# A hybrid decoder trunk on one core: the rectified index scores of a head stay in their bank of PSUM

## The chip, the cores and the metric

The kernel runs on one core of a Trainium2 chip. The metric is the device time of one execution in microseconds. A core has a matrix engine (TensorE, rows "PE" for matmuls and "PEld" for weight loads), an elementwise engine (VectorE, "DVE"), an engine for pointwise functions (ScalarE, "ACT"), a general engine (GpSimd, "POOL") and one that issues most DMAs here (SyncE, "SP"). Each works off its own queue in order and waits for the others at semaphores. SBUF is the working memory; PSUM holds what TensorE writes, in eight banks of 128 partitions x 512 float32.

## The reference, cut to what matters

The model has two layers on an input of 512 tokens x 1024 features. Layer 0 mixes stick-breaking attention with an S5 state space model; layer 1 is a sparse attention that picks 128 keys for each query by an "index score". Each mixer is followed by a squared-ReLU MLP, and both are wrapped as x <- LN(alpha x + f(x)). The change touches the index scores of layer 1:

```python
def block(args):
    q_b, qi_b, wi_b, bid = args
    tpos = bid * Q_BLOCK + jnp.arange(Q_BLOCK)
    rel = jax.nn.relu(jnp.einsum('bqhd,bsd->bqsh', qi_b, ki).astype(jnp.float32))
    score = jnp.einsum('bqsh,bqh->bqs', rel, wi_b.astype(jnp.float32)) * idx_scale
    causal = (spos[None, :] <= tpos[:, None])[None]
    score = jnp.where(causal, score, -jnp.inf)
    _, idx = lax.top_k(score, topk)
```

There are 8 index heads (`IDX_HEADS`) of 32 features, four blocks of 128 queries, and `topk` is 128. The picked keys then go through a softmax attention with 16 heads on 4 key/value heads and a distance penalty (ALiBi).

## The kernel before, in words

All matmuls with weights run three times on a split of each float32 into a high and a low part (`mm3`, L129 to L133). In layer 1 (`mixer_dsa`, L957) the work is issued in this order:

- `index_scores` (L1017) projects the index queries, keys and head weights, carries them through DRAM into the stacked tiles `qist` and `kist`, and calls `score_block` (L1078) for the query blocks 1, 2 and 3. Block 0 needs no choice, since it sees only 128 keys.
- `score_block` handles one block of 128 queries against nk = 256, 384 or 512 keys. For each of the 8 heads TensorE makes one matmul into a bank (`psx`, L1086), ScalarE writes the rectified scores into an SBUF tile `rel` (L1088; the tag has four buffers, and `wiT` in L1062 uses the same tag), and VectorE adds `rel` times the head's weight to the accumulator `acc` in SBUF (L1089). The first addition takes the mask `cm` in place of `acc`.
- `top_keys` (L1114) picks the 128 largest scores of a block on VectorE: 16 steps, each a MAX8 (L1121) and a MATCH_REPLACE8 with its value load (L1122). Then L1126 and L1127 turn the marks into the distance tile `dist`. It is called for block 1, then for block 2, and for block 3 behind the attention of the other blocks in the program's order.
- `project_v1` (L1093) and two `proj_fm` calls make values and keys, and eight `project_q` calls (L1006) make the query pairs. Each `project_q` takes its weights through L104 (ScalarE) and L105 (GpSimd from the third pair on, else VectorE), and its result through L864 and L865 (ScalarE), L866 (GpSimd) and four DMAs (L853) into `qst`.
- `sparse_attention` (L1129) makes the logits of a head (`psl`, L1144), adds the distances on VectorE (L1151, a custom operation that reads `psl` in PSUM and `dist` in SBUF), takes Exp on ScalarE (L1153), scales on GpSimd (L1157), transposes (L944, L945) and sums the values (L951).

The banks: `abank` (L76) hands out four banks of PSUM in turn, three of the tag `psa` and one of the tag `psp`. `psx`, some of the `psi` of the projections, and later `psl`, come from these four. A bank is free again when the last instruction that uses its tile is done. The other four banks (tag `psb`) serve the projections of keys, values and queries.

The order of each engine's queue is not written by hand. The program is traced in the order above, which gives each instruction its priority, and a planner lays out the queues by its own model of time: on every engine the instruction of highest priority whose inputs and buffers are free at that moment goes next. So a queue holds work of several steps mixed: among the projections TensorE finds the matmuls of the scores, and VectorE finds additions between top-k steps. On the chip the queues run in that fixed order.

Of the kernel before, what the change touches and what calls it, by code (L numbers as in the profile page):

```python
# [8 lines left out]
F32 = mybir.dt.float32  # L9
F32R = mybir.dt.float32r  # L10
AF = mybir.ActivationFunctionType
# [4 lines left out]
P = 128  # L16
S = 512
# [18 lines left out]
class Trunk:  # L36
# [1041 lines left out]
    def score_block(self, qb, wi, qst, kst, cm, op, ip):  # L1078

        nc = self.nc  # L1080
        nk = (qb + 1) * P
        qs = slice(qb * P, (qb + 1) * P)
        acc = op.tile([P, S], F32, tag="acc", bufs=3, name=self.nm("acc"))[:, :nk]
        for h in range(8):
            ps = self.abank([P, S], "psx")
            nc.tensor.matmul(ps[:, :nk], qst[:, h, qs], kst[:, :nk], start=True, stop=True)  # L1086
            r = ip.tile([P, S], F32, tag="rel", bufs=4, name=self.nm("rel"))[:, :nk]
            nc.scalar.activation(r, ps[:, :nk], AF.Relu)  # L1088
            nc.vector.scalar_tensor_tensor(acc, r, wi[:, qb, h:h + 1], acc if h else cm[:, S - nk:],  # L1089
                                           ALU.mult, ALU.add)  # L1090
        return acc
# [118 lines left out]
```

## Time and profile before

| | us |
|---|---|
| median of 3 runs (1156.58 to 1158.6) | 1157.38 |
| the profiled execution, its own time | 1157.72 |
| its span, first to last instruction | 1155.9 |
| TensorE matmul busy | 1113.2 (96%) |
| TensorE weight load busy | 928.3 (80%) |
| VectorE busy | 839.0 (73%) |
| ScalarE busy | 532.8 (46%) |
| GpSimd busy | 172.4 (15%) |

The shares are means over stages that differ: what is worth something is read from the stage, from the wait that ends last there. The ends of matmuls are modelled, so a busy TensorE need not be at its peak. The stage that the change touches lies between 606 us (first index score) and some 720 us (last of the top-k steps), in which the DMA engines moved data through more than half of the time up to 680 us. [...]

In the rows, "[7.10 <- X]" says how long the engine stood idle before the row's first instruction and what the profile names as its releaser; "x8" says that eight instructions are merged in the row, which then gives the time from the first start to the last end.

### The profile page before, as it was taken

How to read it: one execution, taken by the hardware profiler on the slowest of the kernel's cores; microseconds unless marked ns; L12 is line 12 of the kernel's file. 1: busy time of each engine (PE TensorE's matmuls, PEld its weight loads, DVE VectorE, ACT ScalarE, POOL GpSimd, SP SyncE). 2: the span in 40 equal slices, each digit the busy share in tenths (PEclk: the TensorE clock that was granted, in tenths of full speed). 3: DMA queues.
4: the chain of work that ended last, by engine and by line, in shares of the span. 5: the costliest groups of instructions: out<-in, count | busy, mean ns of one | idle time of the engine just before them, and what ended most of it. 6: DMA issues, size and time to landing. Idle time of an engine off the chain costs nothing.

```text
span 1155.9 us, 15562 instructions
## 1 busy us (share of the span) xinstructions
PE 1113.2 (96%) x5860; PEld 928.3 (80%) x5860; DVE 839.0 (73%) x1255; ACT 532.8 (46%) x832; POOL 172.4 (15%) x201
## 2 busy tenths in 40 slices
PE   7988999999999999999999979998999999999997
PEld 6877877788888888888898867776988888888886
DVE  7997498695666866975578998556648678587736
ACT  5534387424454544554135446552445444445520
POOL 1043230230000000000121655325000000000001
PEclk9998999999999999999999989998999999999999
DMA  7526683661242242333046960008304405315101
GB/s 247 141 57 155 188 215 117 179 186 38 73 147 90 75 147 71 108 111 79 1 129 159 221 178 1 2 4 271 110 19 128 144 21 162 111 41 160 37 1 73
DMA packets 147307, 126.99 MB, mean 110 GB/s; under 512 B 24353, under 2 KB 115297, under 8 KB 147233
## 3 DMA queue, kind: packets, MB, share of 16 engines
q1 hardware_dynamic: 145552, 123.59, 37.1%
q10 hardware_dynamic: 1680, 2.41, 0.6%
q8 instruction: 46, 0.75, 0.3%
q14 instruction: 29, 0.23, 0.1%
HBM read 105.80 MB, written 5.37 MB: 96 GB/s over the span
## 4 chain that ended last, share of the span: by engine, by line
PE 86%; DVE 7%; DMA 3%; issue 2%; ACT 1%; SPq 1%; POOL 0%; POOLq 0%; DVEq 0%; ACTq 0%
PE psa L132 12%; PE psa L133 12%; PE psa L131 12%; PE psb L313 7%; PE psb L314 7%; PE psb L312 7%; PE pso L951 3%; PE pst L944 3%; PE psb L383 3%; PE psb L382 3%; PE psb L384 3%; PE psb L843 2%; PE psl L1144 2%; PE psb L844 2%; PE psb L845 2%
## 5 line engine op out<-in xcount | busy, mean ns | idle before, releaser
L133 PE MATMUL psa<-xhi,wlo 128*128 128x512 f32 (+1 forms) x720 | 266.9, 371 | 0.0
L132 PE MATMUL psa<-xlo,whi 128*128 128x512 f32 (+1 forms) x720 | 266.6, 371 | 0.0
L131 PE MATMUL psa<-xhi,whi 128*128 128x512 f32 (+1 forms) x720 | 265.2, 371 | 0.2 <-ACT xhi L202 0.2
L104 ACT CAST whi<-raw 128x1024 fp32r<-128x1024 f32 (+1 forms) x129 | 133.6, 1046 | 206.9 <-PE psa L132 127.0
L105 DVE TENSOR_TENSOR wlo<-raw,whi 128x1024 fp32r<-128x1024 f32 (+1 forms) x102 | 128.1, 1260 | 86.8 <-ACT whi L104 86.0
L132 PEld LDWEIGHTS psa<-xlo,whi 128*128 128x128 f32 x720 | 135.7, 188 | 23.3 <-DVE xlo L203 0.4
L133 PEld LDWEIGHTS psa<-xhi,wlo 128*128 128x128 f32 x720 | 135.7, 188 | 22.9
L131 PEld LDWEIGHTS psa<-xhi,whi 128*128 128x128 f32 x720 | 134.8, 188 | 23.3 <-ACT xhi L202 0.5
L313 PE MATMUL psb<-wlo,whi 128*128 128x512 f32 x336 | 130.7, 389 | 0.0
L312 PE MATMUL psb<-whi,whi 128*128 128x512 f32 x336 | 130.7, 389 | 0.0
L300 DVE TENSOR_TENSOR wlo<-b,whi 128x1024 fp32r<-128x1024 f32 x84 | 102.6, 1221 | 38.4 <-ACT whi L299 38.2
L314 PE MATMUL psb<-whi,wlo 128*128 128x512 f32 x336 | 129.8, 389 | 0.0
L299 ACT CAST whi<-b 128x1024 fp32r<-128x1024 f32 x84 | 88.3, 1051 | 41.9 <-PE psb L314 30.2
L105 POOL TENSOR_TENSOR wlo<-raw,whi 128x1024 fp32r<-128x1024 f32 x27 | 69.7, 2592 | 137.8 <-ACT whi L104 136.7
L184 POOL TENSOR_TENSOR rs<-rs,two 128x1 f32<-128x1 f32 x16 | 22.7, 1419 | 418.8 <-DVE rs L183 418.8
L312 PEld LDWEIGHTS psb<-whi,whi 128*128 128x128 f32 x336 | 63.1, 188 | 13.2
L313 PEld LDWEIGHTS psb<-wlo,whi 128*128 128x128 f32 x336 | 63.1, 188 | 13.1
L314 PEld LDWEIGHTS psb<-whi,wlo 128*128 128x128 f32 x336 | 63.1, 188 | 13.0
L294 DVE TENSOR_TENSOR b<-b,b 128x1024 f32<-128x1024 f32 x48 | 58.3, 1221 | 11.1 <-DMA b<-in_w_dram 10.7
L299 ACT CAST whi<-h 128x1024 fp32r<-128x1024 f32 x36 | 37.9, 1054 | 54.0 <-PE psb L313 34.0
L300 DVE TENSOR_TENSOR wlo<-h,whi 128x1024 fp32r<-128x1024 f32 x36 | 44.0, 1221 | 14.0 <-ACT whi L299 13.5
L843 PE MATMUL psb<-whi,xhi 128*128 128x512 f32 x128 | 51.4, 409 | 0.2 <-DVE x L848 0.2
(263 smaller groups left out, 1973.0 us busy)
## 6 DMA issues: line engine op xcount, KB each, us to landing
raw<-in_w_dram SPq DMA_DIRECT2D x80, 512.0 KB, 4.1
b<-in_w_dram SPq DMA_DIRECT2D x48, 512.0 KB, 4.3
raw<-in_w_in_dram SPq DMA_DIRECT2D x29, 512.0 KB, 4.6
raw<-in_w_out_dram SPq DMA_DIRECT2D x16, 512.0 KB, 4.7
qst<-hl SPq DMA_DIRECT2D x48, 128.0 KB, 3.1
kst<-hl SPq DMA_DIRECT2D x24, 256.0 KB, 4.7
gb<-in_ln_g_dram SPq DMA_DIRECT2D x4, 512.0 KB, 4.1
gb<-in_ln_b_dram SPq DMA_DIRECT2D x4, 512.0 KB, 5.1
```

The costliest lines, as they stand in the source:

```text
L104: nc.scalar.copy(hi[:, c], raw[:, c])
L105: (eng or nc.vector).tensor_tensor(lo[:, c], raw[:, c], hi[:, c].bitcast(F32), ALU.subtract)
L131: mm(ps, lhi, rhi, start=start, stop=False)
L132: mm(ps, lhi, rlo, start=False, stop=False)
L133: mm(ps, llo, rhi, start=False, stop=stop)
L294: vec.tensor_tensor(o, p, q, op)
L299: act.copy(hi, src)
L300: vec.tensor_tensor(lo, src, hi.bitcast(F32), ALU.subtract)
L312: mm(ps, lh, bhi[:, k, :], start=i + k == 0, stop=False)
L313: mm(ps, lh, blo[:, k, :], start=False, stop=False)
L314: mm(ps, ll, bhi[:, k, :], start=False, stop=i + k == 2)
L843: nc.tensor.matmul(ps, chi[:, k, tok], whi, start=i == 0, stop=False)
```

## The change

The tile `rel` goes. ScalarE rectifies the scores in place, in the bank that TensorE wrote, and VectorE reads them from there:

```diff
@@ -1084,8 +1084,8 @@
         for h in range(8):
             ps = self.abank([P, S], "psx")
             nc.tensor.matmul(ps[:, :nk], qst[:, h, qs], kst[:, :nk], start=True, stop=True)
-            r = ip.tile([P, S], F32, tag="rel", bufs=4, name=self.nm("rel"))[:, :nk]
-            nc.scalar.activation(r, ps[:, :nk], AF.Relu)
+            r = ps[:, :nk]
+            nc.scalar.activation(r, r, AF.Relu)
             nc.vector.scalar_tensor_tensor(acc, r, wi[:, qb, h:h + 1], acc if h else cm[:, S - nk:],
                                            ALU.mult, ALU.add)
         return acc
```

The numbers of instructions stay as they are: 24 matmuls, 24 rectifications, 24 additions. A bank of `psx` is now in use until VectorE has added it, and no longer until ScalarE has rectified it. The tag `rel` keeps its four buffers, for `wiT`.

## Rows read from the trace of the kernel before

**Rows 1.** From the page, the chain of work that ended last: shares of the span by engine.

```profile
PE 86%; DVE 7%; DMA 3%; issue 2%; ACT 1%; SPq 1%; POOL 0%; POOLq 0%; DVEq 0%; ACTq 0%
```

**Rows 2.** Waits of TensorE's matmuls from 606 to 700 us: in total, times, the longest.

```profile
PE psl L1144 <- DMA qst<-hl: 7.1, 1, 7.1
```

**Rows 3.** The chain of waits from 660 to 700 us: start, us, what.

```profile
684.72 3.98 DMA qst<-hl
688.70 6.24 PE psl L1144 x24
```

**Rows 4.** The timeline from 679 to 690 us, of all engines: start, us, engine, line, operation, tiles, count, and the idle time before with its releaser.

```profile
680.02 1.56 PE L1144 MATMUL psl<-kst,qst 128*128 128x384 f32 x8
688.68 6.26 PE L1144 MATMUL psl<-kst,qst 128*128 128x384 f32 x24 [7.10 <-DMA qst<-hl]
688.68 1.46 PEld L1144 LDWEIGHTS psl<-kst,qst 128*128 128x128 f32 x5 [7.42 <-DVE pst L1151]
...
682.29 1.28 ACT L1153 ACT_TABLE_LOAD   x1
684.22 0.69 DVE L1121 MAX8 top<-acc 128x8 f32<-128x512 f32 x1
685.74 0.69 DVE L1121 MAX8 top<-acc 128x8 f32<-128x512 f32 x1
688.06 0.56 DVE L1151 CUSTOM_DVE_ANT_0 pw<-psl,dist 128x384 f32<-128x384 f32 x1
```

**Rows 5.** All waits of VectorE from 622.5 to 688 us.

```profile
DVE wlo L105 <- ACT whi L104: 0.8, 1, 0.8
```

**Rows 6.** The timeline of VectorE, additions of the scores alone (L1089), blocks 2 (384 keys) and 3 (512 keys).

```profile
627.11 0.61 DVE L1089 SCALAR_TENSOR_TENSOR acc<-rel,wi,acc 128x384 f32<-128x384 f32 x1
627.97 0.60 DVE L1089 SCALAR_TENSOR_TENSOR acc<-rel,wi,acc 128x384 f32<-128x384 f32 x1
...
630.66 2.37 DVE L1089 SCALAR_TENSOR_TENSOR acc<-rel,wi,acc 128x384 f32<-128x384 f32 x1
633.80 0.92 DVE L1089 SCALAR_TENSOR_TENSOR acc<-rel,wi,cm 128x512 f32<-128x512 f32 x1
...
637.03 2.55 DVE L1089 SCALAR_TENSOR_TENSOR acc<-rel,wi,acc 128x512 f32<-128x512 f32 x1
640.88 0.74 DVE L1089 SCALAR_TENSOR_TENSOR acc<-rel,wi,acc 128x512 f32<-128x512 f32 x1
...
643.92 2.54 DVE L1089 SCALAR_TENSOR_TENSOR acc<-rel,wi,acc 128x512 f32<-128x512 f32 x1
```

**Rows 7.** The timeline of GpSimd in the same stretch.

```profile
630.17 2.44 POOL L105 TENSOR_TENSOR wlo<-raw,whi 128x1024 fp32r<-128x1024 f32 x1 [37.21 <-ACT whi L104]
632.57 1.60 POOL L866 TENSOR_TENSOR hl<-ev,hl 128x512 fp32r<-128x512 f32 x1
636.60 2.43 POOL L105 TENSOR_TENSOR wlo<-raw,whi 128x1024 fp32r<-128x1024 f32 x1 [2.42 <-ACT whi L104]
...
643.04 2.88 POOL L105 TENSOR_TENSOR wlo<-raw,whi 128x1024 fp32r<-128x1024 f32 x1 [2.30 <-ACT whi L104]
```

**Rows 8.** The timeline of GpSimd and VectorE from 776 to 800 us.

```profile
786.46 9.09 POOL L105 TENSOR_TENSOR wlo<-raw,whi 128x1024 fp32r<-128x1024 f32 x3 [3.66 <-ACT whi L104]
787.03 2.93 DVE L105 TENSOR_TENSOR wlo<-raw,whi 128x1024 fp32r<-128x1024 f32 x1 [6.36 <-ACT whi L104]
789.88 0.68 DVE L848 SCALAR_TENSOR_TENSOR x<-x,psb 128x512 f32<-128x512 f32 x1
```

**Rows 9.** Four lines of the kernel over the whole span: engine, operation, count, shortest/median/longest in ns, first and last start in us, forms.

```profile
L848 DVE SCALAR_TENSOR_TENSOR x<-x,psb x16: 660/682/689, 179.3 to 812.9; 128x512 f32<-128x512 f32 x16
L105 DVE TENSOR_TENSOR wlo<-raw,whi x102: 683/1222/2927, 6.7 to 1116.9; 128x1024 fp32r<-128x1024 f32 x100, 128x512 fp32r<-128x512 f32 x2
L185 DVE SCALAR_TENSOR_TENSOR x<-x,mv,gb x16: 1271/1276/2425, 233.2 to 1149.7; 128x1024 f32<-128x1024 f32 x16
L1088 ACT ACTIVATE rel<-psx x24: 378/492/606, 607.9 to 639.7; 128x256 f32<-128x256 f32 x8, 128x384 f32<-128x384 f32 x8, 128x512 f32<-128x512 f32 x8
```

**Rows 10.** The timeline of TensorE, the last matmul of a group of four heads, three groups; and of ScalarE, the rectification of the fifth to seventh head of block 3.

```profile
627.96 0.34 PE L1086 MATMUL psx<-kist,qist 96*128 96x384 f32 x1
633.44 0.39 PE L1086 MATMUL psx<-kist,qist 96*128 96x512 f32 x1
638.97 0.40 PE L1086 MATMUL psx<-kist,qist 96*128 96x512 f32 x1
...
637.57 1.74 ACT L1088 ACTIVATE rel<-psx 128x512 f32<-128x512 f32 x3
```

**Rows 11.** The timeline of VectorE, two operations behind the top-k steps.

```profile
648.57 2.60 DVE L1127 TENSOR_TENSOR dist<-acc,drm 128x256 f32<-128x256 f32 x1
670.50 2.35 DVE L1126 TENSOR_SCALAR acc<-acc 128x384 f32<-128x384 f32 x1
```

**Rows 12.** Stretches of the span: length, busy us (and instructions) of TensorE, weight loads, VectorE, ScalarE, GpSimd, then the granted clock, the DMA share and GB/s.

```profile
620.00:640.00 20.00, 20.00 (x98) 16.91 (x97) 19.08 (x39) 14.05 (x25) 7.40 (x4) 1.00 0.54 135
686.00:688.00 2.00, 0.00 (x0) 0.00 (x0) 1.88 (x4) 0.00 (x0) 0.00 (x0) 0.50 0.81 241
...
693.00:694.00 1.00, 1.00 (x7) 1.00 (x6) 1.00 (x6) 0.94 (x4) 1.00 (x2) 0.50 0.00 0
```

## The prediction, made before the result was known

> **What bounds the kernel now.** I read the page's chain of waits first: 86% of it is TensorE's own work, and the profiled execution has a span of 1155.9 us inside its own time of 1157.72 us (1.8 us lie around the span) [rows 1]. So a change can only pay where TensorE stands still. The waits of TensorE between 606 and 700 us show one long one: 7.1 us, in front of the matmuls of the sparse attention (`psl`), put down to a DMA of `qst` [rows 2]. The timeline says otherwise. Eight `psl` matmuls run from 680.02 to 681.58 us and fill the four banks of the score pool; the ninth starts at 688.68 [rows 4]. The chain puts the landing of that DMA at 688.70, after the start it is said to release, and that DMA brings the eighth query pair, while these matmuls read the first four [rows 3]. The weight load of the same moment names VectorE instead, 7.42 us, and VectorE's first `psl` instruction (L1151) begins at 688.06 and ends at 688.62, 0.06 us before TensorE goes on [rows 4]. It frees the first bank. So TensorE waits for VectorE to arrive.
>
> VectorE arrives late because it is full: from 622.5 to 688 us its only wait is 0.8 us [rows 5]. Its queue holds the adding up of the index scores, the top-k steps of blocks 1 and 2, and ten steps of block 3 that the planner put ahead of L1151. Whatever leaves this queue before 688 us moves the attention forward, up to the point where TensorE is the later one: the first two `psl` matmuls are done about 680.5, so at most 7.5 us.
>
> In that queue four of the sixteen score additions of blocks 2 and 3 are stretched. An addition of 128x384 takes 0.60 to 0.61 us and one of 128x512 0.74, but those at 630.66, 637.03 and 643.92 us take 2.37, 2.55 and 2.54, and the one at 633.80 takes 0.92 [rows 6]. Each begins while GpSimd is inside a TENSOR_TENSOR, and the long three end just behind it: 633.03 against 632.61, 639.58 against 639.03, 646.46 against 645.92 [rows 7]. The additions read `rel` and `acc`, both in SBUF.
>
> **The change, part by part.**
>
> *The addition reads PSUM and one SBUF tile.* No row shows this form with a pointer scalar. The nearest is the residual addition L848: same operation, one input in PSUM, 660 to 689 ns, and the one at 789.88 us takes 0.68 in the middle of a GpSimd run of 9.09 us from 786.46, while its neighbour L105, with two inputs in SBUF, takes 2.93 against a median of 1.222 [rows 8, 9]. So I take the stretch as gone: (2.37 - 0.61) + (2.55 - 0.74) + (2.54 - 0.74) + (0.92 - 0.74) = 1.76 + 1.81 + 1.80 + 0.18 = 5.55 us off VectorE's queue. The bounds are 0 (PSUM changes nothing) and 5.55; I take the upper one, since L848 is the same operation under the same GpSimd instruction.
>
> *The unstretched duration.* L848 at 0.682 against 0.735 would make the sixteen additions 16 x 0.05 = 0.8 us shorter; but L848's scalar is an immediate, and a wi column is read per partition. L185, with a pointer scalar, takes 1.276 on 1024 elements where L105 takes 1.222 without one, so 0.05 goes back [rows 9]. I take 0, between -0.8 and +0.8 over the sixteen.
>
> [...]
>
> *The rectifier writes PSUM.* The 24 ScalarE instructions take 378 to 606 ns, PSUM to SBUF [rows 9]; a PSUM output of ScalarE I have no row for. Even 0.1 us either way on each is 2.4 us on an engine that is busy 14.05 of the 20 us from 620 to 640 [rows 12], and the additions behind it wait only where VectorE is already early. I take 0. The four `rel` buffers no longer hold ScalarE back; ScalarE being off the path, that is worth nothing.
>
> *The bank is held longer.* This is the added wait. Before, a bank came free when ScalarE had rectified it; now when VectorE has added it. With four banks, the matmul of head h+4 waits for the addition of head h, and behind it in TensorE's queue stand the projections. Laid against the present order, it hardly bites. The tightest of each four is the last: the eighth matmul of block 2 starts at 627.96, and the addition that would free its bank ends at 627.72; the fourth of block 3 starts at 633.44, where the last addition of block 2, unstretched, ends at 631.27; the eighth starts at 638.97, the addition of the fourth, unstretched, ends at 637.77 [rows 6, 10]. TensorE loses 0 there. VectorE loses something: without stretches it would reach the fifth addition of block 3 at about 640.88 - 3.75 = 637.1, but its rectified bank is only there at 637.57 + 0.6 = 638.17. So 1.07 us of the 5.55 turn into waiting for ScalarE [rows 6, 10]. The planner may place the matmuls earlier or later; between 0 and 2 us lost, I take 1.07.
>
> *Operations that stay stretched.* L1127 and L1126 read SBUF alone; under GpSimd they take 2.60 us at 648.57 and 2.35 at 670.50 [rows 11], some 2 us more each than their size asks for. Moved 4.5 us ahead they begin in another place of GpSimd's rhythm, inside or outside of an instruction. I take 0, between -4 (both free) and +2.
>
> *Sum.* 5.55 - 1.07 = 4.5 us: L1151 begins at about 683.6 and TensorE goes on at 684.2. What is late next is ScalarE: its table load for Exp ends at 683.57, just in time [rows 4]. Everything after follows the same queues in one chain of TensorE pieces, so I let the shift run through to the end. One thing comes on top: the granted clock is 0.50 from 686 to 694 us, after the standstill, and 1.00 from 620 to 640 [rows 12]. The 24 `psl` matmuls behind the standstill take 6.24 us there, where eight took 1.56 at the full clock, which would be 4.7 for 24 [rows 3, 4]; but they also wait for VectorE to free banks, so I expect about 0.5 us of the 1.5 back, between 0 (the clock falls all the same) and 1.5. So 5.0 us: 1157.72 - 5.0 = 1152.7. The profiled execution is 0.34 us above the median of 1157.38 of the runs, so the time is 1152.4 us.
>
> **The rivals.**
>
> *The planner spends the gain (no change).* The order of every queue is written by a planner from its own times. If it thinks VectorE has room before `psl`, it puts more top-k steps of block 3 ahead of L1151. Such a step takes 1.52 us (from one MAX8 at 684.22 to the next at 685.74), and six are left: three more eat 4.6 us, and the time is 1157 [rows 4]. Against it: the stretches look unknown to the planner (L1151 stands where VectorE, without some 10 us of stretches in all, would be at 678, close to `psl`), so removing them need not move its plan.
>
> *The banks become the bound (slower).* Twenty matmuls now wait for an addition. If the planner expects VectorE to be earlier than it is, TensorE stands in front of each. Two such additions start 0.86 us apart (627.11, 627.97) [rows 6]. Its present standstill of 7.1 us is what TensorE can lose before the kernel is slower: 7.1 / 0.86, so from nine matmuls that are reached one step too early, among the sixteen of blocks 2 and 3. With twelve it is 10.3 - 7.1 = 3.2 us: 1160.6. [...] The order of now, laid out above, shows no such early step.
>
> *Half the gain.* One or two steps more ahead of L1151, or PSUM reads that cost 0.05 to 0.1 us more: 5.0 - 2.3 = 2.7, that is 1154.7.
>
> **How the numbers follow.** The forecast gets 0.47, half the gain 0.18, no change 0.19, slower 0.16. A measurement of this kernel tells 0.2% (2.3 us) from no change. Nearly all of the first two cases is faster by more than that, 0.62; same 0.21; slower 0.17. The range reaches down to all of the 7.5 us that VectorE can give back and most of the 1.5 of the clock, 1148.8, and up into the slower case, to 1159.5. The forecast's own range is 1150 to 1154.
>
> **What would show it.** The additions of blocks 2 and 3 all take 0.55 to 0.8 us, those under GpSimd too; L1151 begins about 683.6 and not 688.06; the ninth `psl` follows `psl`'s first eight by under 3 us and not 7.1; the clock falls for a shorter time or not at all. It is wrong if additions from PSUM are stretched as before, if more than ten steps of block 3 stand ahead of L1151, or if TensorE shows waits for `acc` between 620 and 645 us.

## The result, and the profile after

| | before | after |
|---|---|---|
| median (lowest to highest, 4 runs each) | 1157.99 (1156.58 to 1159.16) | 1150.71 (1150.21 to 1152.62) |
| ratio, 95% interval | | 0.9943 (0.9927 to 0.9958) |
| the profiled execution, its own time | 1157.72 | 1151.07 |
| its span | 1155.9 | 1149.3 |
| VectorE busy | 839.0 | 830.8 (72%) |

The change makes the kernel 0.57% faster, 6.6 us between the two profiled executions. The page's chain of waits of the changed kernel, shares of the span by engine, beside [rows 1]:

```profile
PE 88%; DVE 6%; ACT 2%; DMA 1%; issue 1%; SPq 1%; POOL 0%; POOLq 0%; DVEq 0%; ACTq 0%
```

TensorE's share is up by two points and ScalarE's by one, DMA's is down by two; shares of the whole span don't say where the 6.6 us were. That is in the changed kernel's timeline of the stage in front of the attention, all engines, the columns as in [rows 4]:

```profile
680.31 1.91 PE L1144 MATMUL psl<-kst,qst 128*128 128x384 f32 x10
680.86 0.56 DVE L1151 CUSTOM_DVE_ANT_0 pw<-psl,dist 128x384 f32<-128x384 f32 x1 [0.28 <-PE psl L1144]
681.93 1.28 ACT L1153 ACT_TABLE_LOAD   x1
682.55 1.57 PE L1144 MATMUL psl<-kst,qst 128*128 128x384 f32 x6 [0.34 <-DVE pst L1151]
683.23 0.62 ACT L1153 ACTIVATE pw<-pw,pst 128x384 f32<-128x384 f32 x1
...
689.17 0.66 PE L951 MATMUL pso<-pt,v 128*64 128x128 f32 x8 [1.31 <-ACT pt L945]
```

TensorE reaches `psl` at 680.31 (680.02 before), so nothing came from ahead of it. VectorE's L1151 begins at 680.86 and not 688.06, and has now waited 0.28 us for TensorE itself. The standstill of 7.10 us [rows 4] is gone: ten `psl` matmuls run in one piece, and the eleventh waits 0.34. The first Exp begins at 683.23, 0.02 us behind the end of the table load (681.93 + 1.28 = 683.21). Before, it began at 688.66 behind L1151, in the timeline of the kernel before (with its first `pso` matmul, for later):

```profile
688.66 0.62 ACT L1153 ACTIVATE pw<-pw,pst 128x384 f32<-128x384 f32 x1 [5.09 <-DVE pst L1151]
...
696.16 0.66 PE L951 MATMUL pso<-pt,v 128*64 128x128 f32 x8 [0.57 <-ACT pt L945]
```

So 5.43 us of VectorE's 7.2 arrive at ScalarE, and the table load takes the rest. ScalarE is also what ends last behind that. The chain of waits of the changed kernel from 679 to 690 us (start, us, what; "ACT pw" are Exps, each with a read of its sum of 0.19 us behind it):

```profile
681.93 1.28 ACT L1153
...
683.23 0.71 ACT pw L1153 x2
683.94 0.51 ACT hl L865
684.45 4.20 ACT pw L1153 x14
688.65 0.48 ACT pt L945
```

Before, the chain had 6.24 us of TensorE's `psl` matmuls in this place [rows 3]. Now it is ScalarE's table load, eight Exps with one cast of a projection (L865) between them, and a copy, up to the first `pso` matmul.

The additions, in the timeline of the changed kernel's VectorE, for [rows 6]:

```profile
630.36 0.62 DVE L1089 SCALAR_TENSOR_TENSOR acc<-psx,wi,acc 128x384 f32<-128x384 f32 x1 [0.23 <-ACT psx L1088]
...
636.74 0.75 DVE L1089 SCALAR_TENSOR_TENSOR acc<-psx,wi,cm 128x512 f32<-128x512 f32 x1 [0.20 <-ACT psx L1088]
...
643.31 0.75 DVE L1089 SCALAR_TENSOR_TENSOR acc<-psx,wi,acc 128x512 f32<-128x512 f32 x1 [0.40 <-ACT psx L1088]
643.98 0.87 DVE L1126 TENSOR_SCALAR acc<-acc 128x256 f32<-128x256 f32 x1
645.89 0.41 DVE L1127 TENSOR_TENSOR dist<-acc,drm 128x256 f32<-128x256 f32 x1
...
666.69 1.02 DVE L1126 TENSOR_SCALAR acc<-acc 128x384 f32<-128x384 f32 x1
668.24 1.05 DVE L1127 TENSOR_TENSOR dist<-acc,drm 128x384 f32<-128x384 f32 x1
```

And GpSimd in the same time, for [rows 7]:

```profile
629.53 2.41 POOL L105 TENSOR_TENSOR wlo<-raw,whi 128x1024 fp32r<-128x1024 f32 x1 [36.12 <-ACT whi L104]
631.89 1.31 POOL L866 TENSOR_TENSOR hl<-ev,hl 128x512 fp32r<-128x512 f32 x1
635.81 2.41 POOL L105 TENSOR_TENSOR wlo<-raw,whi 128x1024 fp32r<-128x1024 f32 x1 [2.61 <-ACT whi L104]
638.18 1.28 POOL L866 TENSOR_TENSOR hl<-ev,hl 128x512 fp32r<-128x512 f32 x1
642.29 2.41 POOL L105 TENSOR_TENSOR wlo<-raw,whi 128x1024 fp32r<-128x1024 f32 x1 [2.82 <-ACT whi L104]
```

Three additions (630.36, 636.74, 643.31) begin in the middle of a GpSimd subtraction and take 0.62, 0.75 and 0.75 us. Before, such additions took 2.37 to 2.55. Both engines gain: GpSimd's L866 at the first two of these places falls from 1.60 [rows 7] and 1.74 to 1.31 and 1.28. The second of before:

```profile
639.00 1.74 POOL L866 TENSOR_TENSOR hl<-ev,hl 128x512 fp32r<-128x512 f32 x1
```

What the queues wait for. All waits of the matmuls of the changed kernel's TensorE from 618 to 660 us, then VectorE's from 622 to 681 us (in total, times, longest), for [rows 2, 5]:

```profile
PE psx L1086 <- DVE wlo L105: 1.5, 1, 1.5
```

```profile
DVE acc L1089 <- ACT psx L1088: 2.0, 5, 0.7
DVE wlo L105 <- ACT whi L104: 0.5, 1, 0.5
DVE pw L1151 <- PE psl L1144: 0.3, 1, 0.3
```

No matmul waits for `acc`; the one wait, at 621.82, stands ahead of block 2's first scores. VectorE now stands still 2.8 us in all, where it had one wait of 0.8. It is no longer full, and its last wait, in front of L1151, is for TensorE.

One of the stretches of [rows 12] in the changed kernel (the figure behind the five engines is the granted clock of TensorE as a share of its full speed):

```profile
686.00:688.00 2.00, 1.86 (x14) 1.43 (x13) 1.38 (x7) 2.00 (x9) 2.00 (x4) 1.00 0.82 204
```

The clock is 1.00 where it was 0.50 before, and so in every stretch from 606 to 710 us. From the first Exp to the first `pso` matmul it was 688.66 to 696.16, 7.50 us; now it is 683.23 to 689.17, 5.94. As the chain above shows, these 5.94 us are ScalarE's work, no longer TensorE's.

### The profile page after: what moved, and what is told of

It reads as the page before. It is cut to its first block, busy times and chain, and to the rows that moved or that the text cites. A ratio compares the mean times of both kernels' runs of the same rounds, so it can differ in the third digit from the quotient of the medians.

```text
span 1149.3 us, 15542 instructions
## 1 busy us (share of the span) xinstructions
PE 1112.8 (97%) x5860; PEld 926.1 (81%) x5860; DVE 830.8 (72%) x1255; ACT 532.2 (46%) x832; POOL 170.7 (15%) x201
## 3 DMA queue, kind: packets, MB, share of 16 engines
q10 hardware_dynamic: 1680, 2.41, 0.6%
HBM read 105.80 MB, written 5.37 MB: 97 GB/s over the span
## 4 chain that ended last, share of the span: by engine, by line
PE 88%; DVE 6%; ACT 2%; DMA 1%; issue 1%; SPq 1%; POOL 0%; POOLq 0%; DVEq 0%; ACTq 0%
PE psa L133 12%; PE psa L131 12%; PE psa L132 12%; PE psb L313 7%; PE psb L312 7%; PE psb L314 7%; PE pso L951 3%; PE pst L944 3%; PE psb L384 3%; PE psb L383 3%; PE psb L382 3%; PE psb L843 2%; PE psb L844 2%; PE psb L845 2%; PE psl L1144 2%
## 5 line engine op out<-in xcount | busy, mean ns | idle before, releaser
L105 DVE TENSOR_TENSOR wlo<-raw,whi 128x1024 fp32r<-128x1024 f32 (+1 forms) x102 | 128.1, 1260 | 87.3 <-ACT whi L104 86.5
L132 PEld LDWEIGHTS psa<-xlo,whi 128*128 128x128 f32 x720 | 136.2, 189 | 23.5 <-DVE xlo L203 0.4
L105 POOL TENSOR_TENSOR wlo<-raw,whi 128x1024 fp32r<-128x1024 f32 x27 | 69.3, 2576 | 139.0 <-ACT whi L104 137.7
```

The lines of the kernel that those rows point to most:

```text
L105: (eng or nc.vector).tensor_tensor(lo[:, c], raw[:, c], hi[:, c].bitcast(F32), ALU.subtract)
L132: mm(ps, lhi, rlo, start=False, stop=False)
```

## The experiments

Two theories were open. **Theory A**: an addition with two SBUF inputs collides with GpSimd's reads, and a PSUM input ends that. **Theory B**: the gain comes from the new order of the queues, for with other buffers the planner puts eight top-k steps of block 3 ahead of L1151 and not ten, and four steps of block 1 ahead of the first addition of block 2 and not six. (Here and below, steps are counted by their MAX8.)

**e1: the kernel before, GpSimd only writes.** GpSimd's subtractions for six of the query weights (L105) and for the low parts of the keys and queries (L866) become memsets, so these low parts are left out, as in e2.

```diff
@@ weights, L105: only for the query projections from the third pair on
-            (eng or nc.vector).tensor_tensor(lo[:, c], raw[:, c], hi[:, c].bitcast(F32), ALU.subtract)
+            nc.gpsimd.memset(lo[:, c].bitcast(F32), 0.0)
@@ evacuate, L866
-        nc.gpsimd.tensor_tensor(hl[:, 1, :], raw, hl[:, 0, :].bitcast(F32), ALU.subtract)
+        nc.gpsimd.memset(hl[:, 1, :].bitcast(F32), 0.0)
```

> The kernel before, with the rectified scores in SBUF, but GpSimd does not read SBUF beside VectorE: its subtractions for six of the query weights and for the low parts of the keys and queries (L105 in project_q, L866) are memsets to zero, so the low parts of these operands are left out. The order of VectorE's queue stays that of before (ten top-k steps of block 3 ahead of L1151). Theory A (two SBUF inputs of an addition collide with GpSimd's reads): no addition over 0.8 us, L1126 and L1127 short too, about 10 us less on VectorE's queue, of which TensorE can use some 7: L1151 between 680.5 and 681.5 us, time 1150 to 1152. Theory B (the gain of the change comes from the new order of the queues, two top-k steps fewer ahead of L1151): order as before, time within 1.5 us of before.

Measured 1149.86 (1149.36 to 1153.76), ratio 0.9945 (0.9932 to 0.9958). The additions of e1 over the whole span (shortest/median/longest in ns; the lines lie five further down; the first addition of each block, which reads `cm`, has a line of its own, 751 ns at most):

```profile
L1094 DVE SCALAR_TENSOR_TENSOR acc<-rel,wi,acc x21: 476/610/753, 609.1 to 641.2; 128x256 f32<-128x256 f32 x7, 128x384 f32<-128x384 f32 x7, 128x512 f32<-128x512 f32 x7
```

They read `rel` and `acc` in SBUF, the order is that of before (ten steps ahead), and none is stretched, though some meet GpSimd at work. VectorE's timeline, then GpSimd's:

```profile
635.84 0.73 DVE L1094 SCALAR_TENSOR_TENSOR acc<-rel,wi,acc 128x512 f32<-128x512 f32 x1
```

```profile
635.66 0.96 POOL L106 MEMSET wlo<- 128x1024 f32 x1 [5.00 <-PE psa L136]
```

This addition begins and ends inside a memset and takes its 0.73 us, so a GpSimd instruction beside it does not suffice for a stretch; the ones beside the stretched additions read SBUF. The gain is all there without the change. Theory A holds, and the new order isn't needed for the gain. e1 takes the stretches of L1126 and L1127 of blocks 1 and 2 away too (1.60 us in all, 6.28 before), so it doesn't price the additions alone. The edit does more than take the reads away (a memset takes 0.96 us where the subtraction took 2.41, and it waits for no cast), so e2 stands beside it.

**e2: the changed kernel with the same edit.**

> The changed kernel with the same edit of GpSimd (the same low parts left out). Theory A: the additions have nothing left to lose, L1126 and L1127 lose some 2 us of stretch that VectorE does not need any more, since it waits for psl already; time 1150 to 1151.5, equal to the first kernel of this set within 1 us. Theory B: also equal to the changed kernel, 1150.7, but 6 us below the first kernel of this set.

Measured 1150.12 (1149.26 to 1151.14), ratio 0.9941 (0.9928 to 0.9953), the same as the changed kernel and as e1. The two edits don't add up: either of them ends VectorE's lateness, and behind that there is nothing more to gain, as the table below shows. One operation of e2 is still long, and what GpSimd does then tells why; VectorE's timeline, then GpSimd's (L1131 is L1126 of the others; this L108 is L105 of another projection, which kept its subtraction):

```profile
665.26 2.05 DVE L1131 TENSOR_SCALAR acc<-acc 128x384 f32<-128x384 f32 x1
```

```profile
664.23 2.40 POOL L108 TENSOR_TENSOR wlo<-raw,whi 128x1024 fp32r<-128x1024 f32 x1 [4.90 <-ACT whi L104]
```

It ends 0.7 us behind the subtraction (667.31 against 666.63), and in e1 the same operation, outside of one, took 0.36.

**e3: the kernel before, one `rel` buffer.** The additions read SBUF; a rectification waits for the addition before it. This makes the planner lay eight steps ahead of L1151, as in the changed kernel. (`wiT` keeps the tag `rel`, with two buffers.)

```diff
-            r = ip.tile([P, S], F32, tag="rel", bufs=4, name=self.nm("rel"))[:, :nk]
+            r = ip.tile([P, S], F32, tag="rel1", bufs=1, name=self.nm("rel"))[:, :nk]
```

> The kernel before with one rel buffer in place of four (wiT has a tag of its own): five heads in flight and not eight, so the matmuls of the scores come later, and eight top-k steps of block 3 stand ahead of L1151, as in the changed kernel; the additions read SBUF. Theory A: additions under GpSimd take up to 2.6 us again, two to four of them; the two steps fewer give back at most 3.0 us; time 1154 to 1157. Theory B: as the changed kernel, 1150 to 1152.

Measured 1154.55 (1153.08 to 1157.01), ratio 0.9983 (0.9973 to 0.9994). Additions of e3 over the span, and below the longest wait of its matmuls:

```profile
L1089 DVE SCALAR_TENSOR_TENSOR acc<-rel,wi,acc x21: 476/601/2491, 609.6 to 655.0; 128x256 f32<-128x256 f32 x7, 128x384 f32<-128x384 f32 x7, 128x512 f32<-128x512 f32 x7
```

```profile
PE psl L1144 <- DVE pst L1151: 3.9, 1, 3.9
```

The stretches are still there (up to 2.49 us), and the standstill is 3.9 us and not 7.1. The two steps fewer, 3.0 us, are not alone in that: L1126 and L1127 take 3.2 us in all where they took 6.28, and three more steps of block 1 come behind the first addition of block 2. In time this is 0.17%, less than a third of the change's gain. The wait row here names VectorE's L1151 as the releaser, which the DMA label of before hid [rows 2].

**e4: the kernel before, the bank held until the addition.** A write of one column of the bank behind each addition keeps it in use (24 more instructions of 0.06 us on VectorE, so it isn't a clean test of the hold, and additions up to 2.74 us long); nine steps stand ahead of L1151.

```diff
                                            ALU.mult, ALU.add)
+            nc.vector.memset(ps[:, 0:1], 0.0)
```

> The kernel before with the rectified scores in SBUF, and the bank of a head held until its addition by a VectorE memset of one column of the bank behind it (24 small instructions more): four heads in flight as in the changed kernel, nine top-k steps ahead of L1151, almost the changed kernel's order, but SBUF inputs. Theory A: stretched additions as in the kernel before, some 4 to 5.5 us; one step fewer takes 1.5, the memsets add 1 to 1.5: time 1155.5 to 1158.5. Theory B: 1151 to 1153.

Measured 1155.39 (1154.24 to 1156.88), ratio 0.9989 (0.998 to 0.9998). The matmuls' longest wait is again in front of `psl`:

```profile
PE psl L1145 <- DVE pst L1152: 5.4, 1, 5.4
```

With the banks held and SBUF read, most of the standstill stays. Theory B is worth 0.1 to 0.2%, as far as e3 and e4 lay the order as the changed kernel does; ahead of the first addition of block 2 they have three and five steps of block 1, and it has four.

**e5: the kernel before, only block 3 in PSUM.** This halves the dose.

```diff
-            r = ip.tile([P, S], F32, tag="rel", bufs=4, name=self.nm("rel"))[:, :nk]
+            r = (ps if qb == 3 else ip.tile([P, S], F32, tag="rel", bufs=4, name=self.nm("rel")))[:, :nk]
```

> The scores of block 3 alone stay in PSUM; blocks 1 and 2 go through rel in SBUF as before the change. The program then puts nine top-k steps of block 3 ahead of L1151 (ten before the change, eight after it). Theory A (the collision of an addition that reads two SBUF tiles with a GpSimd instruction): the additions of block 3 take 0.72 to 0.75 us all, those of block 2 that fall on a GpSimd instruction still take up to 2.4; 3.8 of the 5.55 us of stretches go, L1151 begins between 682 and 684.5, and the ninth psl matmul follows the first eight by 2 to 4 us; the time is about 4 us below the kernel before, ratio 0.9965, between 0.995 and 0.998. Theory B (only the order of the queues and the held banks count): one step of 1.5 us less ahead of L1151, ratio 0.9985 to 1.

Measured 1149.2 (1148.71 to 1151.7), ratio 0.9939 (0.9924 to 0.9953): the whole gain, where I expected 0.9965, with L1151 between 682 and 684.5 us. VectorE's timeline of e5:

```profile
630.36 2.36 DVE L1089 SCALAR_TENSOR_TENSOR acc<-rel,wi,acc 128x384 f32<-128x384 f32 x1
...
643.21 1.87 DVE L1126 TENSOR_SCALAR acc<-acc 128x256 f32<-128x256 f32 x1
...
646.12 0.40 DVE L1127 TENSOR_TENSOR dist<-acc,drm 128x256 f32<-128x256 f32 x1
...
665.86 1.30 DVE L1126 TENSOR_SCALAR acc<-acc 128x384 f32<-128x384 f32 x1
667.70 1.03 DVE L1127 TENSOR_TENSOR dist<-acc,drm 128x384 f32<-128x384 f32 x1
...
681.45 0.55 DVE L1151 CUSTOM_DVE_ANT_0 pw<-psl,dist 128x384 f32<-128x384 f32 x1
```

Within the stage the theory's part is as expected: the one addition from SBUF that begins inside a GpSimd instruction takes 2.36 us, those from PSUM 0.73 to 0.74. What I left out is the rest of the queue. L1126 and L1127 of blocks 1 and 2 take 4.60 us in all where they took 6.28 (0.29 + 2.60 + 2.35 + 1.04), and the MAX8 of the tenth step, 0.8 us, left the queue ahead of L1151. The first addition of block 2 begins 0.7 us earlier (622.57 against 623.28), and 0.3 us of waiting is new. So 3.8 + 1.7 + 0.8 + 0.7 - 0.3 = 6.7 us, and L1151 is 6.6 us earlier. And the gain saturates, as the table below shows.

**e6: the changed kernel, all scores in one bank**, to price the rival of the banks.

```diff
-            ps = self.abank([P, S], "psx")
+            ps = self.abank([P, S], "psx", True)
```

> The changed kernel with all 24 score matmuls in one single bank, so that each one waits until VectorE has added the head before it. Block 3's additions then spread, and one top-k step of block 3 stands ahead of L1151 instead of eight. If a held bank costs TensorE what the rival of the prediction says, about 0.86 us for each matmul reached too early, then with sixteen or more of them TensorE loses 14 us or more, waits for acc show on TensorE between 607 and 660 us, and the time is above 1160. If TensorE finds projections to do between the matmuls, it loses under 3 us there, L1151 is early in its queue and has no standstill before it, and the time is within 2 us of the changed kernel, 1149 to 1153. I hold the second for likelier, since the order of the queues is planned with the bank known; the additions take 0.60 to 0.75 us in either case.

**e8: the kernel before with the same edit.**

> The kernel before (rectified scores in SBUF) with all 24 score matmuls in the one bank that e6 uses, which every fourth tile of the projections shares. It tells what of e6's loss (1177.15 us against the kernel before's 1156.79) comes from the one bank and what from holding it until VectorE has added. If it is the bank itself, shared with the projections, the score matmuls again stand 6 us apart behind projections, the last ones come after 690 us, and the time is above 1172. If it is the holding (in e6 a matmul, a rectification and an addition follow one another, 1.66 us a head at 384 keys, and 2.4 us at 512 keys with a top-k step in between), each of the sixteen late heads is 0.6 to 1.4 us faster here, and the time is 10 to 20 us below e6, 1157 to 1167. I hold a value between for likeliest, 1165 to 1172.

Measured: e6 1177.15 (1174.94 to 1178.02), ratio 1.0172 (1.0154 to 1.019); e8 1176.95 (1176.36 to 1177.51), ratio 1.0174 (1.0153 to 1.0195). I had held the cheap outcome for likelier in e6, and a value between in e8; both were wrong. Waits of the matmuls from 600 to 720 us, e6 first:

```profile
PE psx L1086 <- DVE acc L1089: 14.8, 10, 1.6
PE psl L1144 <- DVE pst L1151: 7.1, 1, 7.1
PE psl L1144 <- DVE acc L1089: 1.6, 1, 1.6
```

```profile
PE psl L1144 <- DVE pst L1151: 17.3, 1, 17.3
PE psx L1086 <- ACT rel L1088: 6.0, 9, 0.7
...
PE psl L1144 <- ACT rel L1088: 0.7, 1, 0.7
```

In e6 TensorE does lose 14.8 us to held banks, 1.5 us a head. In e8 it loses 6.0. But with the waits in front of `psl` the sums are alike, 14.8 + 7.1 + 1.6 = 23.5 us and 17.3 + 6.0 + 0.7 = 24.0, and L1151 begins at 708.8 and 708.4. In both the scores come late: in e6 single matmuls of block 2 stand 6 us apart between projections (656.03, 662.13, 668.22), and the first of block 3 runs at 682.34 (679.78 in e8), where the kernel before has the fourth at 633.44 [rows 10]. VectorE, which from 669 to 682 us has only single additions, does the sixteen top-k steps of block 2 behind them, and only then L1151. What costs here is one bank for everything; holding it longer added nothing to the time. The granted clock has a mean of 0.62 from 680 to 720 us in both, and of 1.00 from 620 to 680; what part of the 20 us that makes is not shown. That the bank is late because the projections use it too is my reading of the code, not tried by itself.

**e7: L1126 and L1127 made one**, a try at a kernel faster than both.

```diff
-            vec.tensor_scalar(acc, acc, -3.2e38, BIG, ALU.is_gt, ALU.mult)
-            vec.tensor_tensor(dist[:, qb, :nk], acc, drm[:, S - nk:], ALU.max)
+            vec.scalar_tensor_tensor(dist[:, qb, :nk], acc, 3.3e38, drm[:, S - nk:], ALU.add, ALU.max)
```

> The changed kernel with the two operations behind the top-k steps (L1126 and L1127) made one: the accumulator plus 3.3e38, then the larger of that and the masked distance. Three instructions of VectorE go, 0.4 to 1.05 us each, 2 us in all, and nine top-k steps of block 3 stand ahead of L1151 instead of eight. If TensorE is now the later one at L1151 (it waited there 0.28 us for psl), this moves nothing: L1151 at 680 to 681.5 us, the time within 0.1% of the changed kernel, ratio 0.993 to 0.9955 to the kernel before. If VectorE were still what the attention waits for, 1 to 2 us go, ratio 0.992 or below.

Measured 1150.53 (1149.42 to 1151.57), ratio 0.9946 (0.9932 to 0.996): the same as the changed kernel, as expected of a VectorE that is no longer late. From the timeline of e7:

```profile
681.36 0.56 DVE L1150 CUSTOM_DVE_ANT_0 pw<-psl,dist 128x384 f32<-128x384 f32 x1 [0.20 <-PE psl L1143]
```

**All beside each other.** From the timelines: L1151's start, the end of the table load, the first Exp, and the longest standstill inside `psl`.

| | ratio | L1151 | load ends | first Exp | standstill |
|---|---|---|---|---|---|
| before | | 688.06 | 683.57 | 688.66 | 7.10 |
| e4 | 0.9989 | 686.66 | 683.23 | 687.24 | 5.37 |
| e3 | 0.9983 | 684.19 | 682.26 | 684.77 | 3.88 |
| e5 | 0.9939 | 681.45 | 682.67 | 682.68 | 0.73 |
| e7 | 0.9946 | 681.36 | 683.71 | 683.73 | 0.52 |
| after | 0.9943 | 680.86 | 683.21 | 683.23 | 0.52 |
| e1 | 0.9945 | 680.51 | 683.56 | 683.57 | 0.52 |
| e2 | 0.9941 | 680.00 | 682.35 | 682.36 | 0.52 |

In the last five the first Exp follows the table load at once, and their ratios can't be told apart: from there on VectorE may come earlier for nothing. In all five ScalarE works from the first Exp up to the copy in front of the first `pso` matmul with no wait between; in e3 and e4 the first Exp waits for L1151 (2.51 and 4.01 us), as the ninth `psl` matmul does (3.88 and 5.37). In e3 L1151 is only 2.7 us later than in e5, yet the time is 0.44% worse, and the span of the profiled execution 3.6 us longer (1152.2 against 1148.6): 2.1 us are in the first Exp, and 1.3 us come behind it. The granted clock tells that part; e3's stretch (columns as above):

```profile
686.00:688.00 2.00, 2.00 (x7) 1.59 (x6) 2.00 (x9) 2.00 (x7) 1.29 (x1) 0.50 0.41 97
```

Behind its standstill of 3.9 us e3 has half the clock, 0.50: from first Exp to first `pso` it takes 684.77 to 692.09, 7.32 us, nearly the 7.50 of before, and e5, at 1.00 from 682 to 690 us, takes 6.01. How short a standstill can still be followed by the half clock stays open. In front of `pso` the changed kernel stood 1.31 us and e2 1.53, and the clock stayed at 1.00; in the profiled execution of e1 (1153.76 us, its median is 1149.86) the clock fell to a mean of 0.65 from 688 to 690 us, around this wait:

```profile
689.00 1.12 PE L954 MATMUL pso<-pt,v 128*64 128x128 f32 x8 [1.75 <-ACT pt L948]
```

## Why the prediction was right, point by point

The direction and the place were right, and 1150.71 lies 1.7 us under the forecast of 1152.4, inside its range. That the size came out so near is in part luck: VectorE came 7.2 us earlier and not 4.5, the table load took 1.8 of that away, and the stretch behind the first Exp gave 1.6 and not 0.5.

- **The standstill is VectorE's lateness, whatever the label says.** Right: it went when VectorE came earlier, and e3 and e4, with a part of it left, name L1151.
- **The stretch, 5.55 us.** Right: every addition of blocks 2 and 3 takes 0.60 to 0.62 or 0.72 to 0.75 us. L848 was the right row to go by. e1 shows it from the other side: its additions read two SBUF tiles, GpSimd's memsets only write, and no addition takes over 0.753 us.
- **The unstretched duration, 0.** Right: 0.72 to 0.75 against 0.74. The 0.05 to 0.1 us more for a PSUM read, one way to half the gain, was an estimate that no run shows: the longest addition of the changed kernel takes 0.752 us.
- **The rectifier writing PSUM, 0.** Right, or a little on the good side, as one line of the changed kernel over the span shows against [rows 9]:

```profile
L1088 ACT ACTIVATE psx<-psx x24: 364/475/590, 608.0 to 645.6; 128x256 f32<-128x256 f32 x8, 128x384 f32<-128x384 f32 x8, 128x512 f32<-128x512 f32 x8
```

- **The bank held longer.** Right for TensorE: no wait for `acc`. VectorE's wait for ScalarE was taken as 1.07 us and is 2.0, in five additions; under-sized, and without effect, since L1151 still ended 1.8 us ahead of the table load (681.42 against 683.21).
- **"Operations that stay stretched", 0.** This term was mis-sized: L1126 and L1127 of blocks 1 and 2 take 3.35 us (0.87 + 0.41 + 1.02 + 1.05) and not 6.28, so 2.9 us went, inside the bounds that I gave. They still read SBUF, and how long they take goes by where they fall: L1126 of block 1 took 0.29 before, 0.87 after and 1.87 in e5.
- **The planner.** The rival said that it would lay more steps ahead of L1151. It laid fewer. The "ten steps" of the prediction were nine and the MAX8 of a tenth, whose L1122 comes behind L1151, at 689.57; VectorE's timeline of the kernel before:

```profile
687.26 0.69 DVE L1121 MAX8 top<-acc 128x8 f32<-128x512 f32 x1
```

The changed kernel has eight whole steps there, 1.52 + 0.80 = 2.3 us less. It also has one and a half more steps of block 1 behind the first addition of block 2, which take 2.3 us more, counted from start to start. The two cancel: the new order by itself gave VectorE nothing, and I had no case for either. The terms together: -5.55 - 2.9 - 2.3 + 2.3 + 2.1 for waits where there were none = -6.4; from the first addition of block 2 to L1151 it is 622.77 to 680.86, 58.1 us, against 623.28 to 688.06, 64.8 us, so -6.7. The 0.3 between is not assigned. The first addition itself begins 0.5 us earlier, which makes the 7.2.
- **"What is late next is ScalarE: its table load", "just in time".** This is the step that set the size: at 683.21 the load bounds the first Exp, so 5.4 us of the shift pass and not 4.5. The prediction then let "one chain of TensorE pieces" follow; up to the first `pso` matmul the chain is ScalarE's instead.
- **The clock, 0.5 of 1.5.** Under-sized: 7.50 - 5.94 = 1.56, the upper bound. That this is the clock is read from kernels beside each other, e3 and e4 with 7.3 and 7.1 us (a clock of 0.50 from 686 to 688 us) and five with 5.4 to 6.0 (1.00 there), and not tried by itself. It comes whole, since the standstill goes whole, and it ends where ScalarE's chain becomes the longer one (in e1, with no cast between the Exps, that stretch takes 5.43); e3 suggests that with the 683.6 that I forecast for L1151 little of it would have come. So 5.43 + 1.56 = 7.0 us up to `pso`, of which 6.6 are left at the end of the span, against the 5.0 of the sum. An earlier stretch at the lower clock went as well (0.88 before and 1.00 after, the mean of 606 to 620 us), and is worth nothing (e5 has 0.88 there too, and the same time): block 2's first scores run at 621.71 before and at 621.82 after, behind the wait of 1.5 us.
- **The bank rival** did not come. Its price for TensorE was of the right kind (1.5 us a head in e6, 0.86 assumed), but its mechanism isn't what a shortage of banks does here: e8 loses as much without a hold.

## What to carry to other kernels

Before an engine is called slow, look at the same instruction beside and away from another engine's work: rows of one line with durations of 0.74 and 2.54 us point to a collision, and a run in which the other engine only writes can show it (e1, 0.753 us at most). Moving one operand to PSUM ended it here (0.62 to 0.75 us inside GpSimd's subtractions), and no matmul waited for a bank because of that. Then follow the freed time to whatever ends last next; here a table load capped it after 5.4 us, ScalarE's Exps followed, and five different edits that got there gave one time. No run here moved the table load. A standstill may cost more than itself: behind those of 7.10, 5.37 and 3.88 us (before, e4, e3) the clock was 0.50, and the way from the first Exp to `pso` took 7.50, 7.09 and 7.32 us against 5.94.

## What the hardware showed that was not expected

- The collision costs the partner too: with the additions reading PSUM, GpSimd's L866 fell from 1.74 to 1.28 us, with nothing changed in it. In e5 it takes 1.61 us where an addition from SBUF runs beside it and 1.28 where additions from PSUM do.
- A TENSOR_SCALAR with a single SBUF tile collides as well (2.05 us in e2 against 0.36 in e1, under a GpSimd subtraction), which an account by two SBUF inputs alone doesn't cover. No run here takes its cause apart.
- Who starts second pays, in these rows. In e1, VectorE's timeline and then GpSimd's:

```profile
664.65 0.54 DVE L1132 TENSOR_TENSOR dist<-acc,drm 128x384 f32<-128x384 f32 x1
```

```profile
664.75 2.72 POOL L108 TENSOR_TENSOR wlo<-raw,whi 128x1024 fp32r<-128x1024 f32 x1 [2.85 <-ACT whi L104]
670.18 2.41 POOL L108 TENSOR_TENSOR wlo<-raw,whi 128x1024 fp32r<-128x1024 f32 x1 [2.25 <-ACT whi L104]
```

VectorE's operation with two SBUF inputs begins 0.1 us ahead and takes its 0.54; the subtraction behind it takes 0.3 us more than the next one.
